# A hybrid decoder block: the input also comes transposed, and its row blocks are no longer turned by TensorE

## The chip, the cores and the metric

The kernel runs on one core of one Trainium2 chip. The metric is the device time of one execution in microseconds (us). A core has five engines that run their own instruction streams in order: TensorE (PE; its weight loads are shown as PEld), VectorE (DVE), ScalarE (ACT), GpSimd (POOL) and SyncE (SP), which here issues nearly all DMAs. They wait for one another by semaphores.

## The reference, cut to what matters

The block takes x of 4096 tokens by 1024 features in float32. Only its first step is touched by the change:

```
h    = x * rsqrt(mean(x*x, axis=-1) + 1e-6) * attn_norm      # row factor, then a gain per feature
proj = h @ w_in                                              # 1024 x 4104, split into q, k, v, gates, ...
o_a  = gated_delta_net(...)    # heads 0..3, chunks along the sequence
o_b  = retention(...)          # heads 4..7
x    = x + concat(o_a, o_b) @ w_out
out  = final_norm(x + mixture_of_experts(rms_norm(x)))
```

The matrix product needs h with the features on the partitions (the contracted axis), while x lies in memory with the tokens as rows.

## The kernel before

The mixer works through the sequence in 8 superblocks of 512 tokens (T), each made of 4 row blocks of 128 tokens. A superblock has four stages, in the order a1, b1, a0, b0: "a" is a pair of DeltaNet heads, "b" a pair of retention heads, the digit is the pair. A stage has four groups of weight columns; each group's products come in four units, and a unit of a projection is 24 matmuls into one of two PSUM accumulators (`acc`, pool `pa`): 8 slices of the contraction by three terms, since both operands are split into a high and a low part (`hh`, `hl` for the input, `wh`, `wl` for the weights). In `proj_n` the block of 128 tokens is the stationary operand; in `proj_t` the weights are.

Order is written out by hand. After each unit, `unit` runs the steps that `STEPS` lists for its kind: E empties the accumulator (the evacuation), L takes the next step of the DeltaNet chain of the pair before (a generator, `gdn_pair`, whose pace per unit is `PLAN`), B takes one entry of the list `bg`, W and S load or split weights, T runs delayed work. In stage b0 the kinds are r (8 units, here r0 to r7), v (v0 to v3) and y (y0 to y3), with the orders `r="WEBLTS"`, `v="WSBLET"` and `y="WLETSB"`. Every engine takes its part of these steps in the order in which they are written.

Rows of x come in by `x_load` (three buffers `xi`). `x_norm` squares and sums a row block on ACT (L310), finishes the mean on DVE (L311), takes the power on POOL (L312), and returns a closure that multiplies the row block by its row factor and by `attn_norm`, spread over all partitions as `arow` (DVE, L313). `x_turn` turns the block by 8 transposes on TensorE into two PSUM tiles (L320), copies each half into `hh` on ACT (L322), and forms `hl` as the difference on DVE (L323). For the blocks of the next superblock these steps go through `bg`: in b0, `bg` gets `x_norm`, scale for three blocks (six entries, one per unit from r0 on); their `x_turn` come after y1, y2 and y3; the fourth block is normed in units y3 and a0 of the next stage a1 and turned ahead of a1's third projection. The first superblock's rows go through `setup`, between the first four projections.

`split` makes the two parts of a quarter of a weight group (L144 on ACT, L145 on DVE) in the first superblock and stores them in DRAM (`wsp`); later superblocks read them back. After the mixer come the output projection and the experts, which the change leaves alone.

Of the kernel before, what the change touches and what calls it, by code (L numbers as in the profile page):

```python
# [8 lines left out]
F32 = mybir.dt.float32  # L9
# [3 lines left out]
AF = mybir.ActivationFunctionType  # L13
# [4 lines left out]
P = 128  # L18
# [42 lines left out]
def rows(ap, off, pat):  # L61
    return bass.AP(tensor=ap.tensor, offset=ap.offset + off, ap=pat)
# [3 lines left out]
    return ctx.enter_context(tc.tile_pool(name=name, bufs=bufs, reuse_waits="tile", **kw))  # L66


def mixer(tc, outer, banks, x, attn_norm, w_in, conv_a, a_log, dt_bias, norm_a, norm_b, cst, rope, mixed, clear, w_out, x1, wsp):


    nc = tc.nc
# [5 lines left out]
    with ExitStack() as ctx:  # L78
# [8 lines left out]
        ones = C[:, C_UT + P - 1:C_UT + P].to_broadcast([P, P])  # L87
        neg = C[:, C_NEG:C_NEG + P]
        pcol = cp.tile([P, 48], F32, name="pcol")
        arow = mp.tile([P, D], F32, name="arow")  # L90
        nrow = cp.tile([P, 128 + 512 + 8], F32, name="nrow")
        nega = cp.tile([P, 4], F32, name="nega")
        dtb = nrow[:, 644:648]
# [34 lines left out]
        def split(m):  # L128

            if m < len(quarters):  # L130
                src, c0, n, k = quarters[m]
                if m < M0 + 8:
                    t = wp.tile([P, 4 * 264], F32R, name="wq", bufs=NWH)[:, :4 * n]
                    keep = rows(wsp, m % MS * P * 4 * 264, [[4 * 264, P], [1, 4 * n]])
                    h, l = (t[:, 2 * i * n:2 * i * n + 2 * n].rearrange("p (k c) -> p k c", k=2) for i in range(2))
                    whs[m], wls[m] = h, l
                if MS <= m < M0:
                    nc.sync.dma_start(t.bitcast(F32), keep)
                    fetch(m + NWR)
                    return  # L140
                r = raws.pop(m)[:, :, :n]
                if m >= M0 + 8:
                    h, l = (t[:, 2 * k:2 * k + 2, c0 - T:c0 - T + n] for t in out.second)
                nc.scalar.activation(h, r, AF.Copy)  # L144
                nc.vector.tensor_tensor(l, r, h.bitcast(F32), op=OP.subtract)  # L145
                if m < MS and NS > 1:
                    nc.sync.dma_start(keep, t.bitcast(F32))
                if src is w_out and m < M0 + 8:
                    out.first[k, c0 // 256] = h, l
            fetch(m + NWR)  # L150
# [145 lines left out]
            return rest  # L296


        xs = {}

        def x_load(r):
            if r < S // P:
                xs[r] = row()
                nc.sync.dma_start(xs[r], rows(x, r * P * D, [[D, P], [1, D]]))

        def x_norm(r):
            if r < S // P:
                xi, st = xs[r], sp.tile([P, 2], F32, name="st")
                jx = mp.tile([P, D], BF, name="jx", bufs=1)
                nc.scalar.activation(jx, xi, AF.Square, accum_out=st[:, 0:1])  # L310
                nc.vector.tensor_scalar(st[:, 0:1], st[:, 0:1], 1.0 / D, EPS, op0=OP.mult, op1=OP.add)  # L311
                nc.gpsimd.tensor_tensor(st[:, 1:2], st[:, 0:1], ex[:, 0:1], op=OP.pow)  # L312
                return lambda: nc.vector.scalar_tensor_tensor(xi, xi, st[:, 1:2], arow, op0=OP.mult, op1=OP.mult)  # L313

        def x_turn(r):
            i, xi = r % NT, xs.pop(r)
            for q in range(2):
                tr = ptr.tile([P, 4, P], F32, name="tr")
                for j in range(4):
                    nc.tensor.transpose(tr[:, j], xi[:, (4 * q + j) * P:(4 * q + j + 1) * P], ident)  # L320
                sl = (slice(None), slice(4 * q, 4 * q + 4), slice(i * P, i * P + P))
                nc.scalar.activation(hh[sl], tr, AF.Copy)  # L322
                nc.vector.tensor_tensor(hl[sl], tr, hh[sl].bitcast(F32), op=OP.subtract)  # L323

        def next_rows(r):
            if NT <= r < S // P and r in xs:
                x_turn(r)
                x_load(r + NXI)
                if r % NT == 0:
                    bg[:0] = [lambda: None] + x_prep(r + NXI)  # L330

        def x_prep(r):

            box = []
            return [lambda: box.append(x_norm(r)), lambda: box[0] and box[0]()]

        def decays(ba):
            co = gp.tile([P, 14, 16], F32, name="co")
# [53 lines left out]

        L = dict(locals())
        with tc.manual_schedule():
            x_load(0)
            nc.sync.dma_start(ident, cst[:, C_ID:C_ID + P])
            nc.sync.dma_start(arow, rows(attn_norm, 0, [[0, P], [1, D]]))
            nc.gpsimd.memset(ex[:, 0:8], -0.5)
            nc.gpsimd.memset(ex[:, 8:16], 0.5)
            for m in range(NWR):  # L400
# [14 lines left out]
            x_turn(0)  # L415
            for m in range(4):
                split(m)
            scale = x_norm(1)
            split(4)

            def setup(i):

                if i:
                    x_turn(i)
                if i < NT - 1:
                    bg.append(scale if i == 0 else x_norm(i + 1))
                if i == 0:
                    nc.vector.tensor_scalar(nrow[:, :640], nrow[:, :640], 0.5, None, op0=OP.mult)
                    nc.scalar.activation(nega, nrow[:, 640:644], AF.Exp)
                    nc.vector.tensor_scalar(nega, nega, -1.0, None, op0=OP.mult)  # L430
                if i == NT - 1:
                    pp = ptr.tile([P, 512], F32, name="tr")
                    nc.tensor.transpose(pp[:, :48], prow, ident[:48, :48])
                    nc.vector.tensor_copy(pcol, pp[:, :48])
                x_load(i + NXI)
# [1314 lines left out]


def body(tc, x, attn_norm, w_in, conv_a, a_log, dt_bias, norm_a, norm_b, w_out, ffn_norm, wrg, wre,
         w_gate, w_up, w_down, final_norm, cst, rope, cst2, out, parts=7):
    S = x.shape[-2]
    with tc.tile_pool(name="dr", bufs=1, space=DRAM) as dp:
        mixed = dp.tile([S, D], F32, name="mixed")
        x1 = dp.tile([S, D], F32, name="x1")
        tab = dp.tile([NEXP * (S + P), 8], F32, name="tab")
        info = dp.tile([P, 2 * NOV + 1], F32, name="info")
        wsp = dp.tile([64, P, 2, 2, 264], F32, name="wsp")  # L1760
        with ExitStack() as right, ExitStack() as banks, ExitStack() as left:
            o = mixer(tc, left, banks, x, attn_norm, w_in, conv_a, a_log, dt_bias, norm_a, norm_b, cst, rope, mixed, (tab, out),
                      w_out, x1, wsp)
            sh = Shared(tc, pool(tc, right, "sh", 1, side="right"), cst2, ffn_norm, final_norm)
            experts = moe(tc, w_gate, w_up, w_down, sh, x1, tab, info, out)

            def then():
                left.close()
                if parts & 4:
                    next(experts)  # L1770

            if parts & 2:
                post(tc, o, wrg, wre, sh, tab, then)
            banks.close()
            if parts & 4:
                for _ in experts:
                    pass
# [23 lines left out]
```

## Time and profile before

| what | value |
|---|---|
| median of 3 runs | 3530.3 us (3528.6 to 3532.85) |
| the profiled execution | 3531.7 us, of which 3529.9 us is the span from its first to its last instruction |
| TensorE busy | 3373.2 us of the span |
| VectorE busy | 2166.1 us |
| mean granted TensorE clock | 0.986 |

How to read the profile's lines: a timeline line has the start, the length, the engine, the source line, the operation, the tile written and the tile read, the shape and the number of merged instructions; in brackets is the engine's idle time ahead of it and what ended that. Matmuls are pipelined, so their recorded lengths overlap: what one costs is the distance between starts.

### The profile page before, as it was taken

How to read it: one execution, taken by the hardware profiler on the slowest of the kernel's cores; microseconds unless marked ns; L12 is line 12 of the kernel's file. 1: busy time of each engine (PE TensorE's matmuls, PEld its weight loads, DVE VectorE, ACT ScalarE, POOL GpSimd, SP SyncE). 2: the span in 40 equal slices, each digit the busy share in tenths (PEclk: the TensorE clock that was granted, in tenths of full speed). 3: DMA queues.
4: the chain of work that ended last, by engine and by line, in shares of the span. 5: the costliest groups of instructions: out<-in, count | busy, mean ns of one | idle time of the engine just before them, and what ended most of it. 6: DMA issues, size and time to landing. Idle time of an engine off the chain costs nothing. (4 is left out here: it accounts for less than half of the span.)

```text
span 3529.9 us, 64890 instructions
## 1 busy us (share of the span) xinstructions
PE 3373.2 (96%) x24177; PEld 3090.6 (88%) x24177; DVE 2166.1 (61%) x5718; ACT 1502.5 (43%) x3322; POOL 1012.8 (29%) x1320
## 2 busy tenths in 40 slices
PE   7999999999999999999999999999789999999996
PEld 6989999999999999899999988888678888888785
DVE  5685576476466566556655735444556776777775
ACT  4344243233333333333332323222245666766775
POOL 1222232232232222222222211111223444444553
PEclk9999999999999999999999999999889999999998
DMA  8766446455454455464464444323368898899995
GB/s 273 218 241 199 150 152 208 156 161 194 163 184 165 163 175 172 151 206 151 164 209 141 138 157 139 120 97 120 118 203 267 290 314 294 308 325 329 329 321 190
DMA packets 463372, 710.95 MB, mean 201 GB/s; under 512 B 151328, under 2 KB 342480, under 8 KB 463056
## 3 DMA queue, kind: packets, MB, share of 16 engines
q1 hardware_dynamic: 426688, 622.03, 53.4%
q0 software_dynamic: 34976, 84.20, 6.7%
q8 instruction: 191, 3.13, 0.4%
q14 instruction: 125, 1.02, 0.1%
q10 hardware_dynamic: 1392, 0.56, 0.1%
HBM read 606.19 MB, written 131.99 MB: 209 GB/s over the span
## 5 line engine op out<-in xcount | busy, mean ns | idle before, releaser
L243 PE MATMUL acc<-wq,hh 128*128 128x256 f32 (+1 forms) x2560 | 751.1, 293 | 38.5 <-DVE rb L839 23.5
L245 PE MATMUL acc<-wq,hl 128*128 128x256 f32 (+1 forms) x2560 | 724.1, 283 | 2.1 <-DVE hl L323 2.1
L244 PE MATMUL acc<-wq,hh 128*128 128x256 f32 (+1 forms) x2560 | 724.6, 283 | 0.2 <-DVE wq L145 0.2
L243 PEld LDWEIGHTS acc<-wq,hh 128*128 128x128 f32 x2560 | 487.5, 190 | 49.3 <-issue 26.5
L245 PEld LDWEIGHTS acc<-wq,hl 128*128 128x128 f32 x2560 | 485.8, 190 | 2.8 <-DVE hl L323 2.8
L244 PEld LDWEIGHTS acc<-wq,hh 128*128 128x128 f32 x2560 | 487.4, 190 | 0.6 <-DVE wq L145 0.5
L231 PE MATMUL acc<-hh,wq 128*128 128x512 f32 x768 | 317.7, 414 | 0.4 <-DMA wq<-wsp 0.4
L233 PE MATMUL acc<-hh,wq 128*128 128x512 f32 x768 | 302.0, 393 | 0.0
L232 PE MATMUL acc<-hl,wq 128*128 128x512 f32 x768 | 300.9, 392 | 0.0
L1612 PEld LDWEIGHTS g<-xT,gu 128*128 128x128 f32 x2048 | 273.5, 193 | 15.7 <-DVE xT L1544 6.0
L1612 PE MATMUL g<-xT,gu 128*128 128x128 f32 (+30 forms) x2048 | 279.0, 295 | 3.4 <-DVE xT L1544 3.2
L1612 PE MATMUL u<-xT,gu 128*128 128x128 f32 (+30 forms) x2048 | 275.9, 293 | 0.0
L1612 PEld LDWEIGHTS u<-xT,gu 128*128 128x128 f32 x2048 | 266.3, 191 | 1.9
L271 DVE SCALAR_TENSOR_TENSOR cv<-xin,pcol,cv 128x512 f32<-128x512 f32 x288 | 216.3, 751 | 73.5 <-ACT cv L269 66.4
L279 POOL TENSOR_TENSOR gs<-gs,nrow 128x256 f32<-128x256 f32 x128 | 97.0, 758 | 543.6 <-DVE gs L278 517.5
L840 POOL TENSOR_TENSOR rqk<-rqk,rb 128x256 f32<-128x256 f32 x128 | 115.8, 905 | 250.6 <-DVE rb L839 178.9
L966 PE MATMUL y<-dh,hh 128*128 128x512 f32 (+16 forms) x400 | 163.9, 410 | 24.3 <-ACT ys L1555 15.0
L1587 POOL DMA_INDIRECT out_dram<-xg,mi x100 | 131.4, 1314 | 189.7 <-DVE ss L1583 96.3
L1555 ACT ACTIVATE ys<-y,mf 128x512 f32<-128x512 f32 (+22 forms) x200 | 133.8, 680 | 115.1 <-PE y L968 114.2
L233 PEld LDWEIGHTS acc<-hh,wq 128*128 128x128 f32 x768 | 144.2, 188 | 32.9
L1558 POOL DMA_INDIRECT xg<-out_dram,mi x97 | 98.2, 1013 | 255.9 <-PE tr L1542 47.0
L288 POOL TENSOR_TENSOR ss<-ss,ex 128x2 f32<-128x2 f32 x128 | 101.4, 792 | 238.3 <-DVE ss L287 205.1
(375 smaller groups left out, 7905.3 us busy)
## 6 DMA issues: line engine op xcount, KB each, us to landing
wq<-wsp SPq DMA_DIRECT2D x420, 512.0 KB, 5.5
gu<-in_w_gate_dram SPq DMA_DIRECT2D x128, 512.0 KB, 6.4
gu<-in_w_up_dram SPq DMA_DIRECT2D x128, 512.0 KB, 7.9
dn<-in_w_down_dram SPq DMA_DIRECT2D x64, 1024.0 KB, 10.2
xi<-in_x_dram SPq DMA_DIRECT2D x64, 512.0 KB, 5.2
wsp<-wq SPq DMA_DIRECT2D x60, 512.0 KB, 4.3
mixed<-mx SPq DMA_DIRECT2D x128, 128.0 KB, 2.3
out_dram<-zt SPq DMA_DIRECT2D x8, 2048.0 KB, 17.1
```

The lines of the kernel that those rows point to most:

```text
L231: nc.tensor.matmul(a, wh[:, s], hh[:, k, :], start=(k == 0), stop=False)
L232: nc.tensor.matmul(a, wh[:, s], hl[:, k, :], start=False, stop=False)
L233: nc.tensor.matmul(a, wl[:, s], hh[:, k, :], start=False, stop=(k == KC - 1))
L243: nc.tensor.matmul(a[:, :n], hh[:, k, s], wh[:, :n], start=(k == 0), stop=False)
L244: nc.tensor.matmul(a[:, :n], hh[:, k, s], wl[:, :n], start=False, stop=False)
L245: nc.tensor.matmul(a[:, :n], hl[:, k, s], wh[:, :n], start=False, stop=(k == KC - 1))
L271: nc.vector.scalar_tensor_tensor(cv, xin[:, j:j + T], tap(j), cv, op0=OP.mult, op1=OP.add)
L840: nc.gpsimd.tensor_tensor(o.rearrange("p h s d -> p (h s d)"), o.rearrange("p h s d -> p (h s d)"), b.rearrange("p h s d -> p (h s d)"), o ...
L966: nc.tensor.matmul(out, a.hi, b.hi, start=(i == 0), stop=False)
L1555: nc.scalar.activation(self.y[:R, s], y[:R], AF.Copy, scale=self.f[:R, WT, self.n:self.n + 1])
L1587: so = nc.gpsimd.indirect_dma_start(out=orow, out_offset=self.idx(0), in_=self.xg[:self.G], in_offset=None, bounds_check=S - 1, oob_is_err ...
L1612: nc.tensor.matmul(o[:, b, :R], self.w.gu[k // 4][:, k % 4, i * DE + b * P:i * DE + b * P + P], self.xT[:, k, :R], start=(k == 0), stop=(k ...
```

## The change

The host adds `xt`, the same input with each block of 128 tokens transposed: for each block, 128 partitions (feature within a slice of 128) by 8 slices by 128 tokens. `x_load` now reads `xt`. The row factors still need the rows, so `r_load` reads x as well, into one buffer `xr`; each `x_norm` issues the load of the next row block behind its own square. The closure now spreads the 128 row factors over all partitions by one matmul (the factor column, broadcast, against the identity) into a PSUM tile, and multiplies the transposed block by it. `x_turn` only splits. `attn_norm` comes as `acol`, features on partitions, and is multiplied into the weights in `split`, slice by slice. In `bg` the entries of a row block are now `x_norm`, nothing, scale: nine for three blocks in b0, so scales fall on r2, r5 and v0 (before: r1, r3, r5), and the fourth block's entries begin in y2.

```diff
-        arow = mp.tile([P, D], F32, name="arow")
+        acol = cp.tile([P, KC], F32, name="acol")
...
-                nc.scalar.activation(h, r, AF.Copy)
-                nc.vector.tensor_tensor(l, r, h.bitcast(F32), op=OP.subtract)
+                if m < MS:
+                    for i in range(2):
+                        a = acol[:, 2 * k + i:2 * k + i + 1]
+                        nc.scalar.activation(h[:, i], r[:, i], AF.Copy, scale=a)
+                        nc.vector.scalar_tensor_tensor(l[:, i], r[:, i], a, h[:, i].bitcast(F32), op0=OP.mult, op1=OP.subtract)
+                else:
+                    nc.scalar.activation(h, r, AF.Copy)
+                    nc.vector.tensor_tensor(l, r, h.bitcast(F32), op=OP.subtract)
...
-                nc.sync.dma_start(xs[r], rows(x, r * P * D, [[D, P], [1, D]]))
+                nc.sync.dma_start(xs[r], rows(xt, r * P * D, [[D, P], [1, D]]))
+        def r_load(r):
+            if r < S // P:
+                xr[r] = mp.tile([P, D], F32, name="xr")
+                nc.sync.dma_start(xr[r], rows(x, r * P * D, [[D, P], [1, D]]))
...
-                nc.scalar.activation(jx, xi, AF.Square, accum_out=st[:, 0:1])
+                nc.scalar.activation(jx, xr.pop(r), AF.Square, accum_out=st[:, 0:1])
+                r_load(r + 1)
                 nc.vector.tensor_scalar(st[:, 0:1], st[:, 0:1], 1.0 / D, EPS, op0=OP.mult, op1=OP.add)
                 nc.gpsimd.tensor_tensor(st[:, 1:2], st[:, 0:1], ex[:, 0:1], op=OP.pow)
-                return lambda: nc.vector.scalar_tensor_tensor(xi, xi, st[:, 1:2], arow, op0=OP.mult, op1=OP.mult)
+                def scale():
+                    tr = ptr.tile([P, 4, P], F32, name="tr")
+                    nc.tensor.matmul(tr[:, 0], st[:, 1:2].to_broadcast([P, P]), ident, start=True, stop=True)
+                    xi = xs[r].rearrange("p (k t) -> p k t", k=KC)
+                    nc.vector.tensor_tensor(xi, xi, tr[:, 0:1].to_broadcast([P, KC, P]), op=OP.mult)
+                return scale
         def x_turn(r):
-            i, xi = r % NT, xs.pop(r)
+            i, xi = r % NT, xs.pop(r).rearrange("p (k t) -> p k t", k=KC)
             for q in range(2):
-                tr = ptr.tile([P, 4, P], F32, name="tr")
-                for j in range(4):
-                    nc.tensor.transpose(tr[:, j], xi[:, (4 * q + j) * P:(4 * q + j + 1) * P], ident)
-                sl = (slice(None), slice(4 * q, 4 * q + 4), slice(i * P, i * P + P))
-                nc.scalar.activation(hh[sl], tr, AF.Copy)
-                nc.vector.tensor_tensor(hl[sl], tr, hh[sl].bitcast(F32), op=OP.subtract)
+                k = slice(4 * q, 4 * q + 4)
+                sl = (slice(None), k, slice(i * P, i * P + P))
+                nc.scalar.activation(hh[sl], xi[:, k], AF.Copy)
+                nc.vector.tensor_tensor(hl[sl], xi[:, k], hh[sl].bitcast(F32), op=OP.subtract)
...
-                    bg[:0] = [lambda: None] + x_prep(r + NXI)
+                    bg[:0] = x_prep(r + NXI)
...
-            return [lambda: box.append(x_norm(r)), lambda: box[0] and box[0]()]
+            return [lambda: box.append(x_norm(r)), lambda: None, lambda: box[0] and box[0]()]
...
+            r_load(0)
+            nc.sync.dma_start(ident, cst[:, C_ID:C_ID + P])
+            nc.sync.dma_start(acol, rows(attn_norm, 0, [[1, P], [P, KC]]))
             x_load(0)
-            nc.sync.dma_start(ident, cst[:, C_ID:C_ID + P])
-            nc.sync.dma_start(arow, rows(attn_norm, 0, [[0, P], [1, D]]))
...
-            scale = x_norm(1)
+            scales = [x_norm(1)]
             split(4)
             def setup(i):
                 if i:
                     x_turn(i)
-                if i < NT - 1:
-                    bg.append(scale if i == 0 else x_norm(i + 1))
+                if scales:
+                    scales.pop(0)()
+                if i + 2 < NT:
+                    scales.append(x_norm(i + 2))
```

## Rows read from the trace of the kernel before

**Rows 1.** The page, part 1: busy time, share of the span, instructions.
```profile
PE 3373.2 (96%) x24177; PEld 3090.6 (88%) x24177; DVE 2166.1 (61%) x5718; ACT 1502.5 (43%) x3322; POOL 1012.8 (29%) x1320
```
**Rows 2.** Busy time by stretch (us, instructions), then granted clock, DMA share, GB/s.
```profile
0.00:44.00 44.00, 25.15 (x131) 22.61 (x132) 19.86 (x34) 15.66 (x29) 5.81 (x17) 0.88 0.82 273
44.00:258.00 214.00, 206.53 (x1464) 192.12 (x1463) 163.30 (x426) 98.35 (x261) 53.74 (x76) 0.98 0.73 234
...
1538.00:1794.00 256.00, 252.38 (x1906) 237.80 (x1906) 157.57 (x452) 90.04 (x276) 67.59 (x103) 1.00 0.53 170
```
**Rows 3.** Waits of TensorE from 44 to 2030 us: total, times, longest.
```profile
PE acc L243 <- DVE rb L839: 23.5, 18, 2.2
PE acc L243 <- DVE gs L278: 6.7, 8, 3.1
```
**Rows 4.** Timeline of TensorE, units y0 to y3 of b0, seventh superblock.
```profile
1766.00 0.61 PE L882 MATMUL sm<-qkt 128*128 128x128 f32 x4
1766.37 0.37 PE L243 MATMUL acc<-wq,hh 128*128 128x256 f32 x1
...
1767.88 1.03 PE L320 MATMUL tr<-id,xi 128*128 128x128 f32 x8
1769.25 0.39 PE L243 MATMUL acc<-wq,hh 128*128 128x256 f32 x1 [0.34 <-DVE gs L278]
...
1774.43 1.04 PE L320 MATMUL tr<-id,xi 128*128 128x128 f32 x8
1775.22 0.36 PE L243 MATMUL acc<-wq,hh 128*128 128x256 f32 x1
```
**Rows 5.** Timeline of VectorE, units r5 to y0 of the same b0.
```profile
1745.15 0.37 DVE L836 TENSOR_TENSOR rqk<-acc,rt 128x256 f32<-128x256 f32 x1
...
1745.84 1.26 DVE L313 SCALAR_TENSOR_TENSOR xi<-xi,st,arow 128x1024 f32<-128x1024 f32 x1
1747.04 0.70 DVE L723 TENSOR_SCALAR tk<-tk 128x8 f32<-128x8 f32 x1
...
1749.78 0.41 DVE L836 TENSOR_TENSOR rqk<-acc,rt 128x256 f32<-128x256 f32 x1
...
1750.50 2.88 DVE L732 SCALAR_TENSOR_TENSOR V<-U,V 128x31 f32<-128x31 f32 x12
...
1768.81 0.38 DVE L278 SCALAR_TENSOR_TENSOR gs<-th,acc 128x256 f32<-128x256 f32 x1
```
**Rows 6.** Timeline of the last superblock's b0, VectorE, then TensorE.
```profile
1996.12 0.15 DVE L723 TENSOR_SCALAR tk<-tk 128x8 f32<-128x8 f32 x1
...
2019.47 0.39 PE L243 MATMUL acc<-wq,hh 128*128 128x256 f32 x1 [1.63 <-DVE gs L278]
```
**Rows 7.** Timeline of the first 44 us.
```profile
11.87 0.59 PE L243 MATMUL acc<-wq,hh 128*128 128x264 f32 x1 [1.22 <-ACT wq L144]
...
13.11 0.34 SPq L410 DMA_DIRECT2D cst<-in_cst_dram  x1
...
14.41 1.06 ACT L310 ACTIVATE jx<-xi 128x1024 bf16<-128x1024 f32 x1 [0.65 <-DMA xi<-in_x_dram]
...
15.83 0.54 POOL L312 TENSOR_TENSOR st<-st,ex 128x1 f32<-128x1 f32 x1 [8.60 <-DVE st L311]
...
33.40 0.39 PE L243 MATMUL acc<-wq,hh 128*128 128x264 f32 x1 [0.52 <-ACT hh L322]
...
43.70 0.40 PE L231 MATMUL acc<-hh,wq 128*128 128x512 f32 x1
```
**Rows 8.** DMA time to landing of the row loads, first 50 us.
```profile
DMA to landing us min/median/max: 3.3/5.6/9.5
```
**Rows 9.** VectorE lines L145 and L323: length in ns min/median/max, first and last start.
```profile
L145 DVE TENSOR_TENSOR wq<-wr,wq x51: 671/686/1268, 60.3 to 252.8; 128x512 fp32r<-128x512 f32 x51
L323 DVE TENSOR_TENSOR hl<-tr,hh x64: 674/681/693, 10.5 to 1797.1; 128x512 fp32r<-128x512 f32 x64
```
**Rows 10.** Timeline of TensorE, first superblock's b0, start of y2.
```profile
262.25 0.39 PE L243 MATMUL acc<-wq,hh 128*128 128x256 f32 x1 [3.08 <-DVE gs L278]
```

More of the change, by code (lines that the diff above doesn't have):

```diff
@@ L66, in pool, with mixer @@
     return ctx.enter_context(tc.tile_pool(name=name, bufs=bufs, reuse_waits="tile", **kw))
-def mixer(tc, outer, banks, x, attn_norm, w_in, conv_a, a_log, dt_bias, norm_a, norm_b, cst, rope, mixed, clear, w_out, x1, wsp):
+def mixer(tc, outer, banks, x, xt, attn_norm, w_in, conv_a, a_log, dt_bias, norm_a, norm_b, cst, rope, mixed, clear, w_out, x1, wsp):
     nc = tc.nc
@@ L296, in norm_out @@
             return rest
-        xs = {}
+        xs, xr = {}, {}
         def x_load(r):
@@ L303, in x_load @@
                 xs[r] = row()
-                nc.sync.dma_start(xs[r], rows(x, r * P * D, [[D, P], [1, D]]))
+                nc.sync.dma_start(xs[r], rows(xt, r * P * D, [[D, P], [1, D]]))
[3 more added lines that the diff above has]
+                nc.sync.dma_start(xr[r], rows(x, r * P * D, [[D, P], [1, D]]))
         def x_norm(r):
             if r < S // P:
-                xi, st = xs[r], sp.tile([P, 2], F32, name="st")
+                st = sp.tile([P, 2], F32, name="st")
@@ L1752, in body @@
 def body(tc, x, attn_norm, w_in, conv_a, a_log, dt_bias, norm_a, norm_b, w_out, ffn_norm, wrg, wre,
-         w_gate, w_up, w_down, final_norm, cst, rope, cst2, out, parts=7):
+         w_gate, w_up, w_down, final_norm, cst, rope, cst2, xt, out, parts=7):
     S = x.shape[-2]
@@ L1761, in body @@
         with ExitStack() as right, ExitStack() as banks, ExitStack() as left:
-            o = mixer(tc, left, banks, x, attn_norm, w_in, conv_a, a_log, dt_bias, norm_a, norm_b, cst, rope, mixed, (tab, out),
+            o = mixer(tc, left, banks, x, xt, attn_norm, w_in, conv_a, a_log, dt_bias, norm_a, norm_b, cst, rope, mixed, (tab, out),
                       w_out, x1, wsp)
@@ L1791 @@
     arrays["cst2"] = constants2()
+    arrays["xt"] = np.ascontiguousarray(arrays["x"].reshape(S // P, P, KC, P).transpose(0, 3, 2, 1))
     arrays = {f"in_{n}_dram": a for n, a in arrays.items()}
```

## The prediction

> **What bounds the kernel now.** I read the busy times first, then busy time by stretch, then TensorE's own waits, and last the timeline where those waits fall. TensorE is busy for 96% of the span, VectorE for 61% [rows 1]: the first guess is that every microsecond taken from TensorE is a microsecond won. The stretches qualify that. A middle superblock has 256 us with 252.4 us of TensorE work at the full granted clock [rows 2], so some 3.6 us of idle time per superblock; the first 44 us hold only 25.2 us of work. TensorE's waits between 44 and 2030 us are nearly all for VectorE, to empty an accumulator [rows 3]. In the timeline the first kind sits in the r units (r7 waits for r5's accumulator in most superblocks), the second at y2, which starts 0.34 us after TensorE was ready, on the gate product `gs` of y0 [rows 4]. So there is a stretch in each b0, from the middle of the r units to the start of y2, whose length is set by VectorE; outside it, TensorE sets the pace. Both kinds of stretch hold a part of the change.
>
> **Price of the turns.** Eight transposes move the next projection by 0.79 us (1774.43 to 1775.22), and the first matmul behind a switch is recorded about 0.08 us longer: 0.87 us [rows 4]. A float32 matmul of the new one's shape shows as two records; four records take 0.37 us to the next start, with the switch 0.46 us, so one costs 0.23 us [rows 4]. On TensorE alone a row block gains 0.64 us; the 28 blocks behind the first superblock 17.9 us. That is one bound.
>
> **The steady state, block by block.** There are seven sets of four blocks, one per change of superblock.
>
> *Blocks two and three* are turned after y2 and y3, where VectorE is not late: minus 2 x 0.87 = 1.74 us. *Block four* is turned ahead of the third projection of a1: minus 0.87; its new matmul stands behind a1's first projection and is not covered: plus 0.23. The matmuls of blocks one to three stand behind r2, r5 and v0, inside the stretch that VectorE sets; their 0.69 us hides behind the waits of r7 and y2, and would be added if those waits were gone.
>
> *Block one* is turned after y1, just ahead of the start of y2, which waits for VectorE anyway [rows 4]. Taking these 0.87 us away only lengthens that wait; the last superblock, which has no such turn there, shows it: y2 waits 1.63 us instead of 0.34 [rows 6]. So y2 starts when `gs` of y0 is done, and VectorE is at work without a gap from r7's evacuation at 1749.78 to there, 1768.81 [rows 5]. What does the change do to this chain? The third scale moves from r5 to v0, into it. The r5 place is taken by the second scale, so r6 and r7 gain nothing and the chain grows by one multiplication, 1.26 us [rows 5]; the new one has the same 1,024 elements per partition, and I take that price. The third block's mean falls behind r6: 0.15 us more, the price of L723 [rows 6] as the nearest tiny operation. Against that, L723 took 0.70 us behind the old scale [rows 5] and 0.15 where no scale precedes it [rows 6]. The delay looks like a lock with POOL: the old scale reads two SBUF tensors, holds up POOL's sum of r5, and that sum holds up L723. The new scale reads one operand from PSUM; I take back 0.4 of the 0.55 us. Together y2 starts 1.0 us later; bounds 0.4 and 1.4.
>
> One set is then -1.74 - 0.87 + 0.23 + 1.0 = -1.38 us, seven sets -9.7 us. The bounds are -17.9 us (the chain is no limit) and, with 1.4 us on the chain and one blocked `hl` (next), -0.4 us a set: -2.7 us.
>
> `hl` now subtracts two SBUF tensors, where one came from PSUM. L145 has two and took up to 1.268 us where 0.686 is its median; L323, one from PSUM, stays within 0.693 [rows 9]. So up to 0.58 us can be added when POOL works at the same time. In y2 and y3 VectorE has room for it; ahead of a1's fourth projection it could reach TensorE: between nothing and 0.58 us a set. I take nothing, since the subtraction no longer waits for a turn and has the whole third projection, 24 matmuls, to run in. The Trainium skill says of this, in "SBUF — State Buffer", section "Who interferes with whom", that a VectorE instruction with two SBUF inputs contends with a GpSimd instruction that reads SBUF, and that the later one blocks. The trace agrees (1.268 against 0.693 us). By that rule alone, every fourth block's subtraction being caught, the seven sets would give -5.6 us in place of -9.7.
>
> **The first superblock.** Its 64 splits become two instructions each on ACT and VectorE. A half costs at least 0.38 us (the gate product of 256 columns [rows 5]), two 0.8 against 0.69 [rows 9]: about 0.13 us per split. This is hidden behind TensorE except in the stretches that VectorE sets: some eight splits in b1 and nine in b0, 1.0 and 1.2 us. In b0 y2 waits 3.08 us already [rows 10], so nothing there can be covered. Plus 2.2 us, bounds 0 and 4.
>
> **The start.** Before, the first projection began at 11.87 [rows 7], while the norm of block one came later and off TensorE's queue. Now the spreading matmul of block one stands in TensorE's queue ahead of that projection, and it needs the rows of block one, whose load SP issues behind all the setup loads (13.11 is the last [rows 7]), at 13.5 or later. It lands 5.6 us later by the median of such loads [rows 8], at about 19.5. From the square's start to the end of the power it takes 1.96 us (14.41 to 16.37 [rows 7]): the matmul runs at about 21.5, the projection ends near 27. Block two's rows are loaded only after block one's square and behind the stores of the split weights, near 21, landing near 27; its matmul is ahead of the second projection, which so starts near 30. Block three's load follows block two's square, lands near 33.5, and its matmul can run near 35.5, in front of the third projection; by the pace of projections and splits this comes at 37.5, where it was 33.40 before [rows 7]. From there on the pace is the old one: the transposed products begin at about 48 instead of 43.70 [rows 7]. Queued behind the waiting squares on ACT are the evacuations and splits, already counted; behind `r_load` on SP, which waits for each square, the next weight loads. Plus 4.5 us. With 3.3 us for each landing the same chain gives +0.5, with 9.5 us +12 [rows 8]. The load of `acol` (4 KB in pieces of 4 bytes) is covered by the wait for block one's rows; without this cover it would be on the way of the first split.
>
> In the steady state the doubled input (16.8 MB more) goes into queues at half their share [rows 2] and lands within three units, some 9 us; ACT has room. I cost it at nothing; if a load were later than that, ACT would stand in its square and the evacuations of the v and y units behind it.
>
> **The sum.** -9.7 + 2.2 + 4.5 = -3.0 us against the profiled execution's 3531.7 us: 3528.7. That execution lies 1.4 us above the median of the runs, so I forecast 3527.3 us.
>
> **Rivals.** 0.2% is 7 us, about what a measurement of this kernel can tell from no change.
>
> *TensorE is the bound everywhere*: VectorE's chain has slack that I don't see (a cheaper scale, fewer locks with POOL), and the four turns pay in full. For it: 96%. Against it: y2's waits [rows 4, 6, 10]. -17.9 + 4.5 + about 1 = -12.4: 3518 us, faster.
>
> *The start decides against it*: each of the three row loads lands as late as the latest, since the queues are full in the first 44 us (share 0.82 [rows 2]): +12 there, and the chain in b0 at its upper bound, -2.7 + 4: +13, 3543 us, slower. It decides from landing times of some 8 us on, with the chain at that bound. Against it: the median of 5.6.
>
> *VectorE's chain takes nearly all*: y2 is 1.4 us later and `hl` blocked, with the start as forecast: -2.7 + 2.2 + 4.5 = +4, 3534 us, no change that can be told.
>
> **Chances.** My forecast 0.40, TensorE everywhere 0.27, the chain takes all 0.18, the start 0.15. Some of the forecast's own spread reaches past -7 us (about 0.08), and some of the start's stays under +7. Faster by over 0.2%: 0.33; within: 0.49; slower: 0.18. The likeliest case's own range is 3522 to 3533; the range that takes in the rivals, but not the whole of the start's, is 3515 to 3540 us.
>
> **What would show it.** Right: y2's wait for `gs` grows from 0.34 us to about 2.2; y3 and a1 follow with no turn; a superblock is shorter by 1.4 us; the 512-column products begin at 46 to 50 us, TensorE's first projection near 21. Wrong: superblocks shorter by 2.5 us, or y2's start not tied to `gs` of y0; a start before 45 us; new waits of TensorE for POOL (row factors) or of ACT for the row load in the middle.

## The result, and the profile after

The changed kernel takes 3559.65 us (median of 6 runs, 3557.07 to 3564.64), the kernel before 3530.1 us beside it: a ratio of 1.0083, 95% interval 1.0072 to 1.0094. It is 29.5 us slower; the forecast was 3527.3 us, with 3540 us as the upper end.

The page of the changed kernel, part 1, answers to [rows 1]:

```profile
PE 3370.9 (95%) x23985; PEld 3084.7 (87%) x23985; DVE 2180.8 (61%) x5782; ACT 1521.2 (43%) x3386; POOL 993.0 (28%) x1320
```

TensorE is busy for 2.3 us less and the kernel is 30 us longer, so most of the loss lies in waits; busy time also grows where the granted clock is lower, since the same products then take longer (in the first stage, matmuls of 264 columns start 0.22 us apart at a clock of 0.50 and 0.12 us apart at 1.00). VectorE, which had slack, has 15 us more to do. Busy time by stretch, cut at the changed kernel's own stages, answers to [rows 2]:

```profile
0.00:56.00 56.00, 22.39 (x106) 20.41 (x107) 20.49 (x41) 18.15 (x37) 6.63 (x17) 0.85 0.80 260
56.00:280.00 224.00, 209.40 (x1477) 194.16 (x1477) 178.75 (x491) 113.60 (x319) 51.93 (x77) 0.98 0.74 237
1552.00:1808.00 256.00, 249.15 (x1864) 234.27 (x1862) 158.31 (x453) 88.91 (x270) 63.53 (x100) 0.99 0.55 178
```

The first stage is 12 us longer with less TensorE work in it. A middle superblock, where 1.4 us less was forecast, has more idle time than before, and its granted clock is 0.99 where it was 1.00. TensorE's waits from 56 to 2040 us say for whom (total, times, longest; before in [rows 3]):

```profile
PE acc L250 <- DVE rb L859: 21.4, 19, 2.4
PE acc L238 <- DMA wq<-wsp: 21.1, 6, 4.1
PE acc L250 <- DVE gs L285: 16.6, 8, 4.5
```

The third line is the wait at y2, longer by 10 us in all, as forecast. The second is new: before, the first 512-column product waited for weights once, for 0.4 us in all; now it waits in six of the eight superblocks, 3.5 us on average. The forecast had no such wait.

**A ledger.** Two moments stand in both traces: the first 512-column product (L231 before, L238 after) and the start of y2 in each b0.

| from, to | before | after | difference | forecast |
|---|---|---|---|---|
| begin to the first 512-column product | 43.70 | 55.94 | +12.2 | +4.5 |
| to y2 of the first superblock (262.25; 279.35) | 218.6 | 223.4 | +4.9 | +2.2 |
| to y2 of the last, seven superblocks (2019.47; 2057.31) | 1757.2 | 1778.0 | +20.7 | -9.7 |
| the rest of the span | 1510.4 | 1505.5 | -4.9 | 0 |

The sum is +32.9, the two profiled executions' difference (3564.64 and 3531.7 us). The change touches nothing in the last row's work, and I have no cause for its 4.9 us; over the traces of this case that do the whole computation it lies between 1500.6 and 1510.4 us, and the kernel before with only its fills moved has 1507.4. The third row is the one to explain.

**Where the new wait comes from.** SyncE's timeline in a1 of the seventh superblock. The first fence is the kernel before, which was not shown for this engine; there y2 started at 1518.27:

```profile
1532.20 0.33 SPq L304 DMA_DIRECT2D xi<-in_x_dram  x1
...
1533.06 0.56 SPq L632 DMA_DIRECT2D tab<-zt  x1
1533.67 5.66 SPq L632 DMA_DIRECT2D out_dram<-zt  x1
1539.37 11.04 SPq L138 DMA_DIRECT2D wq<-wsp  x4
```

The same place in the changed kernel, where y2 started at 1556.91:

```profile
1572.76 0.33 SPq L311 DMA_DIRECT2D xi<-in_xt_dram  x1
...
1573.62 0.56 SPq L652 DMA_DIRECT2D tab<-zt  x1
1574.23 5.67 SPq L652 DMA_DIRECT2D out_dram<-zt  x1
1579.99 11.15 SPq L138 DMA_DIRECT2D wq<-wsp  x4
```

SyncE's order is the same: the next row block (`x_load`), the rope table, the zero fills of `tab` and `out_dram`, the weights of a1. Only the head comes later: 15.9 us behind y2 instead of 13.9. `x_load` waits until the buffer `xi` of block three is free. Before, its last reader was the transpose; now it is VectorE's subtraction `hl`, which ends later. The timelines show it, TensorE before, then VectorE in the changed kernel:

```profile
1531.13 1.04 PE L320 MATMUL tr<-id,xi 128*128 128x128 f32 x8
```

```profile
1570.87 1.86 DVE L340 TENSOR_TENSOR hl<-xi,hh 128x512 fp32r<-128x512 f32 x2
```

The turns end at 1532.17 and the load goes out at 1532.20; the subtractions end at 1572.73 and the load goes out at 1572.76. (The profile's table of SyncE's waits puts this wait, 4.1 us, down to the product `Sb` at L895. That began at 1572.66 and ended at 1573.07, behind the load's issue, so it cannot have released it.)

So the load of a block that is wanted a superblock later holds up the fills, and the fills stand ahead of weights that are wanted at once. TensorE, meanwhile, is ready earlier: it begins the first 512-column product 32.1 us behind this y2, where it was 34.3 before. It meets the missing weights here:

```profile
1593.21 0.50 PE L238 MATMUL acc<-hh,wq 128*128 128x512 f32 x1 [2.59 <-DMA wq<-wsp]
```

and pays again behind it. In the busy time by stretch of these microseconds the column to read is the granted clock, the number behind the last bracket:

```profile
1592.00:1594.00 2.00, 0.79 (x3) 0.67 (x4) 0.00 (x0) 0.00 (x0) 0.00 (x0) 1.00 0.98 379
1594.00:1596.00 2.00, 2.00 (x9) 1.69 (x7) 0.00 (x0) 0.00 (x0) 0.00 (x0) 0.53 1.01 346
1596.00:1598.00 2.00, 2.00 (x8) 1.62 (x7) 1.54 (x8) 0.00 (x0) 0.00 (x0) 0.61 1.06 406
1598.00:1600.00 2.00, 2.00 (x13) 1.70 (x12) 1.69 (x11) 0.29 (x1) 0.00 (x0) 1.00 1.02 416
```

TensorE stands still for 2.6 us and then runs near the lower level (1.2 GHz) for most of 4 us: about 1.7 us more lost (0.47 and 0.39 of 2 us each). The Trainium skill describes this pattern in "TensorE: Matmul & The Clock Gate", section "HAM oscillation — how this bites in real kernels": a wait for a transfer between groups of matmuls is paid a second time by a slow start of the next group. The rows here agree.

The last superblock of the same trace is a check: no row block is left to load there, the fills go out 12.6 us behind y2 instead of 16.7 to 18.3, and TensorE does not wait for weights.

### The profile page after: what moved, and what is told of

Same layout as the page of the kernel before. It is cut to its first block, busy times and chain, and to the rows that moved or that the text cites. A ratio compares the mean times of both kernels' runs of the same rounds, so it can differ in the third digit from the quotient of the medians.

```text
span 3562.8 us, 64769 instructions
## 1 busy us (share of the span) xinstructions
PE 3370.9 (95%) x23985; PEld 3084.7 (87%) x23985; DVE 2180.8 (61%) x5782; ACT 1521.2 (43%) x3386; POOL 993.0 (28%) x1320
## 5 line engine op out<-in xcount | busy, mean ns | idle before, releaser
L238 PE MATMUL acc<-hh,wq 128*128 128x512 f32 x768 | 323.5, 421 | 21.1 <-DMA wq<-wsp 21.1
L240 PE MATMUL acc<-hh,wq 128*128 128x512 f32 x768 | 306.0, 398 | 0.0
L238 PEld LDWEIGHTS acc<-hh,wq 128*128 128x128 f32 x768 | 147.9, 193 | 50.4 <-DMA wq<-wsp 23.7
L240 PEld LDWEIGHTS acc<-hh,wq 128*128 128x128 f32 x768 | 146.9, 191 | 34.2
L239 PEld LDWEIGHTS acc<-hl,wq 128*128 128x128 f32 x768 | 148.1, 193 | 25.6
```

Of the source, the lines that this page charges most:

```text
L238: nc.tensor.matmul(a, wh[:, s], hh[:, k, :], start=(k == 0), stop=False)
L239: nc.tensor.matmul(a, wh[:, s], hl[:, k, :], start=False, stop=False)
L240: nc.tensor.matmul(a, wl[:, s], hh[:, k, :], start=False, stop=(k == KC - 1))
```

## The experiments

The theory (A): in the steady state the loss is the late release of `xi`, through SyncE's order, and nothing else; without it the forecast's -1.4 us per superblock is there. The main rival (B): the second input copy loads the queues so much that weights come late wherever they stand. A second question is the start, a third what is left to win. The kernel before was run again beside each group of runs, with medians from 3526.64 to 3529.11 us; each ratio is to the median beside it. In the texts written ahead of the runs, e1 is the changed kernel with the fills out of the way, e3 the one with the load behind the fills, f1 the one with the rows ahead.

**The fills out of the way**, in the changed kernel and, as control, in the kernel before:

```
-  if (kind, pr) == (("a", 1) if sb else ("a", 0)):
+  if (kind, pr) == (("b", 1) if sb else ("a", 0)):
```

> The changed kernel with one line different: from the second superblock on, the zero fills of the output and the table are issued at the start of stage b1 instead of a1. Theory A (late weights): SP's load of the next transposed block now waits for VectorE's subtraction of block three; the 2.5 MB of fills and then the weights of a1's first 512-column group stand behind it on SP, so TensorE waits some 3.5 us there in six superblocks and then runs some microseconds at the lower clock. Then both go: the six waits (21.1 us) are gone, the middle superblocks take 249.3 us instead of 255.0, the kernel 3525 us (3520 to 3530). Rival B (the second row load and SP's waits for the squares are the load): the fills are not the cause, at least half of the waits stay, 3545 us or more. Rival C (the loss per superblock is VectorE's chain at y2): the superblocks stay at 255, 3560 us.

> The kernel before with the same move of the zero fills, as a control. A: there the weights came just in time (one wait of 0.4 us in all), so moving the fills gives nothing: 3530 us, within 2 us. If moving the fills by itself were worth tens of microseconds, e1 would not speak for A: then 3510 or less.

Measured: the changed kernel 3530.34 us against 3526.64 beside it (ratio 1.0008, 0.9999 to 1.0018), the kernel before with the same edit 3530.53 us (1.001, 1.0001 to 1.002). Of the 29.5 us, 3.7 are left, and the interval of the ratio takes in 1; the time is just above the 3520 to 3530 us that was expected. TensorE's waits for weights fall from 21.1 to 1.2 us, and the six superblocks between the first y2 and the seventh take 249.7 us instead of 255.0. The control shows that moving the fills is no gain by itself (they then hold up weights in the last superblock's b1, 1.7 us of waits in its trace). With the same edit, the two kernels are level.

**The load behind the fills**, which keeps the fills where they were:

```
+ if r % NT == 2: held.append(r + NXI)
+ else: x_load(r + NXI)
  ...
  for t in clear: zero(nc, t, zt, sb, NS)
+ while held: x_load(held.pop())
```

> The changed kernel; the fills stay at a1, but the load that waits for block three's subtraction is issued behind them. Same DMAs, same bytes, another order on SP. A: the fills and the weights no longer wait for VectorE, the six waits go, 3527 us (3520 to 3533). B: nothing changes, since the same bytes are moved: 3560 us.

Measured: 3528.55 us (ratio 1.0007, 0.9997 to 1.0016). SyncE in the seventh superblock's a1; the y2 before it was at 1522.79:

```profile
1536.91 0.56 SPq L658 DMA_DIRECT2D tab<-zt  x1
1537.52 5.42 SPq L658 DMA_DIRECT2D out_dram<-zt  x1
1543.04 9.58 SPq L312 DMA_DIRECT2D xi<-in_xt_dram  x1
1552.72 1.82 SPq L138 DMA_DIRECT2D wq<-wsp  x4
```

The fills go out 14.1 us behind y2 instead of 16.7 (12.6 to 14.2 over the superblocks), and the last weights' issue ends 31.8 us behind it instead of 34.2, though a load now stands between them. No wait of TensorE for weights is left before 2080 us. The seven superblocks from y2 to y2 take 1743.9 us: 13.3 less than before, 34.1 less than in the changed kernel. That is 13 us more than the 21.1 us of waits, and the granted clock is where they were: in the changed kernel, stretches of 8 us from each of the six waits on had a mean clock of 0.57 (four times) or 0.79 (twice). The share that is missing adds up to 17 us, a part of it while TensorE still stood, which covers the 13. The edit keeps every transfer and every byte; only the order on SyncE is another.

**The kernel before without the turns.** The eight transposes are left out and ACT and VectorE split the untransposed rows, so the numbers are others; no second layout, no second load, 256 transposes fewer:

```
- for j in range(4):
-     nc.tensor.transpose(tr[:, j], xi[:, (4 * q + j) * P:(4 * q + j + 1) * P], ident)
+ tr = xi[:, 4 * q * P:(4 * q + 4) * P].rearrange("p (k t) -> p k t", k=4)
```

> The kernel before with its 256 turns simply left out (the split reads the rows where they are, so the products are those of other numbers); no second load, no spreading matmul, scales where they were. It shows what taking the turns away is worth at most. A: block buffers are released by the subtraction here too, so the weights of a1 come late as well: waits of 2 to 3.5 us in the middle superblocks and a lower clock behind them; of the 24 us of turns little is left, 3520 to 3540 us. B: without the second load no waits, 3508 us.

Measured: 3546.76 us (ratio 1.005, 1.0033 to 1.0067): slower, with work taken away and nothing added. TensorE's waits, 60 to 2080 us,

```profile
PE acc L231 <- DMA wq<-wsp: 22.0, 6, 4.4
```

and VectorE and SyncE ahead of the seventh superblock's fills, the y2 before them at 1540.73:

```profile
1555.73 1.29 DVE L321 TENSOR_TENSOR hl<-xi,hh 128x512 fp32r<-128x512 f32 x2 [0.36 <-ACT hh L320]
1557.05 0.33 SPq L304 DMA_DIRECT2D xi<-in_x_dram  x1
```

`x_load` now goes out when `hl` ends, as in the changed kernel, 16.3 us behind y2, where it went out when the transposes ended before, and the wait for weights appears in full, six times, with one input copy: B falls. The time is 7 us above A's own range. And y2 waits 1.1 to 1.3 us instead of 0.34, as the forecast said of a turn taken from ahead of y2: the time only moves into the wait.

**The rows ahead.** From here each kernel contains the load behind the fills unless it says otherwise. The rows of blocks one to three go early into tiles that are idle then (`at`, `X`, `U`), and each is loaded ahead of its transposed block:

```
+ early = {1: ('at', 8), 2: ('X', 8), 3: ('U', 8)}
  ...
  for r in range(1, min(NXI, NT)):
+     r_load(r)
      x_load(r)
```

> The kernel of e3 (late load behind the fills) with the rows of blocks one to three loaded early at the start, into buffers that are idle then, each ahead of its transposed block, instead of each behind the square of the block before. Theory A (the start is lost to three row loads in series): the first 512-column product begins at 44 to 48 us instead of 55.9, and the kernel is 8 to 11 us faster than e3, some 3519 us. Rival B (the start is lost to split weights, to the bytes themselves or to the clock): the start stays above 52 us and the time within 3 us of e3.

Measured: 3524.05 us (ratio 0.9985, 0.9975 to 0.9994), 4.5 us less than without, or 6 by the kernel before beside each; the first 512-column product begins at 49.67 instead of 52.96. That is about half of what was expected, and the timelines of ACT and TensorE say why:

```profile
22.73 0.91 ACT L148 ACTIVATE wq<-wr,acol 128x256 fp32r<-128x256 f32 x2 [7.52 <-DMA wr<-in_w_in_dram]
23.55 1.04 ACT L328 ACTIVATE jx<-X 128x1024 bf16<-128x1024 f32 x1
...
26.21 0.79 PE L338 MATMUL tr<-id,st 128*128 128x128 f32 x2 [4.90 <-POOL st L334]
```

Block two's rows, issued at 7.25, are no longer what the square waits for; it stands on ACT behind a split of weights, for which ACT stood idle 7.5 us. The wait was pushed from one load to the next.

**The scale one entry earlier.** Block scales sit two entries of the work list behind their norms, and the third falls into VectorE's chain ahead of y2. This puts them one entry behind, and the empty entry in front of the list:

```
- return [lambda: box.append(x_norm(r)), lambda: None, lambda: box[0] and box[0]()]
+ return [lambda: box.append(x_norm(r)), lambda: box[0] and box[0]()]
- bg[:0] = x_prep(r + NXI)
+ bg[:0] = [lambda: None] + x_prep(r + NXI)
```

> The kernel of e3 with the empty entry taken out between norm and scale, so that the scales fall on r1, r3 and r5 as before the change. Theory A (the third scale at v0 lengthens VectorE's chain ahead of y2): y2's wait falls from 1.93 us to 0.9 to 1.3 us and the kernel gains 4 to 7 us on e3, 3523 us. Rival B (the matmul then waits for the power on POOL, one unit earlier): TensorE gets waits for POOL of about a microsecond, three per superblock, and the gain is gone or turned: 3528 us or more.

Measured: 3563.14 us (ratio 1.0102, 1.0085 to 1.0119): 35 us slower than without, a plain miss. TensorE's waits, 60 to 2080 us, and SyncE ahead of the seventh superblock's fills (the y2 before them at 1555.02):

```profile
PE acc L238 <- DMA wq<-wsp: 21.2, 6, 4.8
PE tr L330 <- POOL st L326: 19.2, 8, 3.3
PE acc L250 <- DVE gs L285: 13.7, 9, 4.5
```

```profile
1569.50 0.33 SPq L317 DMA_DIRECT2D xr<-in_x_dram  x1
...
1570.36 0.56 SPq L658 DMA_DIRECT2D tab<-zt  x1
```

y2 waits 1.1 us instead of 1.9, the gain meant. Two things cost more. The spreading matmul, now straight behind the norm, waits 2.5 us for GpSimd's power once in each superblock. And the empty entry moved a row load behind one more square; it holds the fills until 15.3 us behind y2 instead of 14.1, and the six waits for weights are back. The same fault as in the change, made by another load. To part the two costs, the same edit on the changed kernel with the fills in b1, so that no fill stands ahead of those weights:

> The changed kernel with each block's scale one entry of the work list behind its norm, as in the run that put the scales there (3563.1 us), but with the zero fills in the next group of products instead of the first 512-column group (as in the run with the fills moved, 3530.3 us). Question: why did the scale one entry earlier cost 35 us? Theory A, two parts: (1) the empty entry in front moved a row load behind a square and with it the fills (1.2 us later against y2) and the weights (six waits, 21.2 us together, each with some us of low clock behind it: about 34 us by the runs with and without these waits); (2) TensorE now waits 2.5 us once in a superblock at the spreading matmul for GpSimd's power and 0.8 us less at y2. Here (1) is gone and (2) stays: no wait of TensorE for wq over 1.5 us before 1800 us, 7 to 8 waits of 2.5 us for st, y2 waits of 1.1 us, superblocks of 250.5 to 251.5 us, 3538 us (3533 to 3543). Theory B (the waits for GpSimd's power are all of it): 3560 us. Theory C (the weights are all of it, the 2.5 us are given back): 3525 us, superblocks of 248.5.

Measured: 3538.85 us (ratio 1.0031, 1.002 to 1.0041), by theory A 3538. The same waits, 60 to 2080 us:

```profile
PE tr L329 <- POOL st L325: 19.2, 8, 3.3
...
PE acc L250 <- DMA wq<-wsp: 2.8, 3, 1.8
```

The waits for GpSimd stay, those at L238 go, and 24 of the 35 us with them. The rest is 8.5 us over the kernel with the fills moved alone by the medians, and 9.3 between the first and the last y2 of the traces (1755.4 and 1746.1). Seven times 2.5 less 0.8 would be 12; why some of it does not show was not looked into.

**The splits as before**, with attn_norm left out of the weights, so that the numbers are others; the later stages depend on them (the whole took 3740.3 us, which compares with nothing), and only the first superblock is read:

```
- if m < MS:
+ if False:
```

> The kernel of e3 with the weights split as before, in one instruction on each engine; attn_norm is left out of the computation. It prices the gain in the weights. Theory A: 0.13 us for each of some seventeen splits that lie in the stretches set by VectorE in the first superblock: 2.2 us faster than e3, the wait of y2 there 3.3 us instead of 4.47. Rival B: the split is hidden altogether, the wait stays at 4.4 us.

Measured: from the first 512-column product to y2 of the first superblock 217.0 us (57.11 to 274.10), against 223.6 us with the split halves; TensorE's waits there are 11.0 us instead of 14.8. Busy time by stretch, with the split halves, then without:

```profile
52.96:276.54 223.58, 208.77 (x1474) 193.54 (x1472) 178.56 (x490) 113.09 (x317) 50.56 (x76) 0.98 0.74 237
57.11:274.10 216.99, 206.01 (x1473) 190.75 (x1472) 165.76 (x434) 98.07 (x261) 51.45 (x76) 1.00 0.76 243
```

So the split halves cost 6.6 us there, where the forecast had 2.2: 3.8 us of waits, and 2.8 us more of TensorE's busy time for the same products, at a granted clock of 0.98 instead of 1.00. The wait of y2 fell only to 4.12 us, not to the 3.3 expected; the rest of the 3.8 lies in the waits ahead of it. Against the kernel before (218.6) the rest of the change gives back 1.6 us.

**The norms in a0.** With the rows ahead, the norms and scales of the next superblock's first three blocks start from a0 instead of b0, one stage earlier and away from VectorE's chain:

```
  gs = []
+ if pr == 0:
+     for r in range(min(NXI, NT)): bg += x_prep(4 * sb + 4 + r)
  ...
- if pr == 0:
-     for r in range(min(NXI, NT)): bg += x_prep(4 * sb + 4 + r)
```

> The kernel of f1 with the norms and scales of the next superblock's first three blocks moved from stage b0 to stage a0. Theory A (VectorE sets the length of b0 from the r units to y2): with three scales and means out of it, the waits of r7 and y2 shrink, the middle superblocks take 247 us or less instead of 249.3, and the kernel is 10 to 18 us faster than f1, some 3505 us. Rival B (a0 has no room, its convolutions fill VectorE): TensorE gets new waits in a0 and nothing is won.

Measured: 3518.18 us (ratio 0.9971, 0.9959 to 0.9982): faster than the kernel before and the changed one, but 5.9 us under the run with the rows ahead, where 10 to 18 were expected; the six middle superblocks take 248.6 us, not 247. TensorE's waits, 60 to 2080 us:

```profile
PE acc L250 <- DVE rb L874: 15.2, 12, 2.4
PE acc L250 <- DVE gs L285: 13.0, 9, 3.8
PE acc L250 <- DVE tk L758: 8.6, 8, 2.4
PE acc L238 <- DMA wq<-wsp: 2.7, 2, 1.4
```

The waits for `gs` and `rb` fall by 11.5 us against the run with the rows ahead (18.2 and 21.5), and 7.7 us of that come back as waits for `tk`. With the fills in b1 on top:

> The fastest version so far (rows of the first blocks early, the load behind the fills, the norms of the next superblock begun in a0: 3518.2 us) with the zero fills in the next group of products as well. Theory A (a weight load that waits behind the fills costs the wait and a low clock behind it): the two waits of 1.3 us for wq that are left there go, 3515 us (3511 to 3519). Theory B (they cost nothing more than 2.7 us, or the fills hurt in their new place too): 3518 us or more, with waits for wq in b1.

Measured: 3516.13 us (ratio 0.9963, 0.9949 to 0.9976). The waits at L238 are gone, 2.3 us of others stand in b1; the two versions can't be told apart, their intervals overlap.

## Why the prediction was wrong

**The step that failed** is the price of the removed turns together with that of the loads in the steady state. The transposes were priced as TensorE's time alone; they were also what set `xi` free, and their removal put the release on VectorE's `hl`. The loads were put at nothing ("I cost it at nothing; if a load were later than that, ACT would stand in its square"): that sentence asked whether bytes find room in the queues, and where a late load would be missed. It didn't ask what a load itself waits for, and what stands behind it on SyncE. The forecast named what is queued behind `r_load`'s wait, and not what is behind `x_load`'s. In place of nothing the traces showed six waits for weights, 21.1 us together, and about 13 us more at the lower clock behind them; the times put it at 27.6 us of the 29.5: the changed kernel is 29.5 us above the kernel before beside it, the one with the load behind the fills 1.9. The kernel before without its turns shows the same waits without the rest of the change, so the second input copy is not their cause.

**The steady state without this step: the sum right, its pieces in part by luck.** With the load behind the fills a superblock takes 249.1 us on average against 251.0: -1.9 us, forecast -1.4, bounds -0.4 to -2.6. Cut at two waits of TensorE for `rb` that stand in both traces, the long one in b1 and the one at r7 of b0 (means over the superblocks):

| from, to | before | load behind the fills | difference | forecast |
|---|---|---|---|---|
| y2 to the long wait in b1 | 104.4 | 102.8 | -1.5 | -2.4 |
| to r7 of b0 | 123.8 | 122.8 | -1.0 | 0 |
| to y2 | 23.0 | 23.6 | +0.6 | +1.0 |

The first row holds the turns of blocks two to four. In four of the seven superblocks it is 102.1 to 102.4 us, close to the forecast; in the other three the granted clock falls behind y2, whose wait is now longer, and 1.5 us are lost, a term that the forecast didn't have. In the second row "r6 and r7 gain nothing" failed. VectorE behind r3 and TensorE at r7 in the seventh superblock, before:

```profile
1735.79 2.62 DVE L665 SCALAR_TENSOR_TENSOR E<-E,co,cst 128x128 f32<-128x128 f32 x4
1746.06 0.36 PE L243 MATMUL acc<-wq,hh 128*128 128x256 f32 x1 [1.55 <-DVE rb L839]
```

and with the load behind the fills:

```profile
1739.60 1.62 DVE L691 SCALAR_TENSOR_TENSOR E<-E,co,cst 128x128 f32<-128x128 f32 x4
1748.97 0.36 PE L250 MATMUL acc<-wq,hh 128*128 128x256 f32 x1 [0.64 <-DVE rb L865]
```

The same four products take 1.0 us less where no scale stands ahead of them at r3, and r7's product starts earlier by as much: the forecast counted such a delay for L723 behind r5, and not for these. So y2 starts 0.4 us earlier against the wait in b1, where 1.0 us later was forecast, while the first row gained less than forecast; that the two nearly cancel is luck. Other pieces, in the timelines of VectorE and TensorE, b0 of the changed kernel's sixth superblock:

```profile
1541.57 1.21 DVE L331 TENSOR_TENSOR xi<-xi,tr 128x1024 f32<-128x1024 f32 x1
...
1556.91 0.39 PE L250 MATMUL acc<-wq,hh 128*128 128x256 f32 x1 [1.90 <-DVE gs L285]
```

The third scale stands inside VectorE's chain, as said, at 1.21 us (price taken: 1.26); the product behind the old scale's place takes 0.15 to 0.23 us where 0.70 stood in [rows 5], so about all of the 0.55 us came back, not 0.4; and y2 waits 1.90 us, forecast 2.2. The rival that TensorE sets the pace everywhere falls with this wait. `hl` with two SBUF operands was caught more often than "every fourth": its mean is 0.92 us with the load behind the fills (54 subtractions between 280 and 2000 us, up to 1.27 us), where L323 had 0.693 at most in [rows 9]. Of the 54, 27 take 0.83 us or more, and each of them overlaps an instruction of GpSimd in the trace; the 20 that overlap none take 0.68. But no wait of TensorE for it shows behind the start, so "nothing" was right for its price.

**The first superblock: a term too small.** +4.9 us, forecast +2.2 with bounds 0 and 4. The split was priced by the gate product at 0.38 us a half (twice that is 0.76, which against 0.69 gives 0.07 us per split, not the 0.13 written). Measured, by groups of the changed kernel from 0 to 280 us, VectorE:

```profile
L149 DVE SCALAR_TENSOR_TENSOR wq<-wr,acol,wq 128x256 fp32r<-128x256 f32 x120 | 58.3, 529 | 12.8 <-ACT wq L148 12.8
```

Two halves on VectorE take 1.06 us, where the whole took 0.76 on average before (the 60 of the same stage), so 0.30 us per split, not 0.13; by the forecast's own 17 uncovered splits that is 5.1 us, and the run with the splits as before measured 3.8 us of waits and 2.8 at a lower clock, 1.6 of which other parts of the change give back. The nearest row read one operand from PSUM, and these read two from SBUF: their median is 0.48 us, so the row taken was already too cheap. The longest half is 0.97 us. The section of the Trainium skill that the prediction weighed for `hl` ("SBUF — State Buffer", "Who interferes with whom") bears on this instruction too, since it has two operands in SBUF. The trace agrees: the 12 halves of 0.95 to 0.97 us all overlap an instruction of GpSimd, and the 81 that overlap none take 0.53 us at most.

**The start: its order right, its size off.** +12.2 us, forecast +4.5, bounds +0.5 and +12. The rival on the start had this price, but by three late loads, and only one of the three was late. The changed kernel's first 56 us, SyncE, ACT and TensorE:

```profile
14.03 0.33 SPq L316 DMA_DIRECT2D xr<-in_x_dram  x1
18.95 1.06 ACT L322 ACTIVATE jx<-xr 128x1024 bf16<-128x1024 f32 x1 [5.27 <-DMA xr<-in_x_dram]
20.96 0.80 PE L329 MATMUL tr<-id,st 128*128 128x128 f32 x2 [13.51 <-POOL st L325]
21.65 0.82 SPq L316 DMA_DIRECT2D xr<-in_x_dram  x1
31.23 1.06 ACT L322 ACTIVATE jx<-xr 128x1024 bf16<-128x1024 f32 x1 [8.83 <-DMA xr<-in_x_dram]
33.42 0.79 PE L329 MATMUL tr<-id,st 128*128 128x128 f32 x2 [7.70 <-POOL st L325]
...
43.22 0.39 PE L250 MATMUL acc<-wq,hh 128*128 128x264 f32 x1 [1.82 <-ACT hh L339]
```

Block one goes as written: issue 14.03 (13.5 said), matmul 20.96 (21.5). Block two is issued at 21.65 (21) and its square starts 9.6 us later, at 31.23, where 27 was said: the longest landing of [rows 8], not the median. Block three's load lands nearly in time: ACT waits 0.9 us for it. From there the third projection begins at 43.22 instead of 37.5, and the products 12.7 us behind it, not 10.3 as before. "By the pace of projections and splits" failed there, since the pace has the granted clock in it: it was 1.00 from 34 us on before, and in the changed kernel, whose projections stand between waits, it is 0.50 from 34 to 40 us, 0.53 from 46 to 48 and 0.50 from 52 to 54.

The first 512-column product's time is 52.5 to 57.6 us in the changed kernel and its versions that load rows as it does, so up to 5 us of the 12.2 vary from one execution to another.

**The sum with measured terms**, for the version with the load behind the fills: +9.3 at the start, +5.0 in the first superblock, -13.3 in the seven others is +1.0 us. The rest of its span is 6.7 us shorter than before, again without a cause that I know, so the two profiled executions differ by -5.8 us, while its median stands 1.9 us above the kernel before. So without the failed step no change could have been told, and the time would have been in the likeliest case's own range; but the three terms were each off by 3 to 5 us and cancelled, which is luck.

## What to carry to other kernels

When an instruction is removed, ask what it released: the buffer's next load now waits for the next-later reader, and everything issued behind that load on the same queue is late with it, even transfers that the change doesn't touch. Price a moved or added load three times: its bytes, what it waits for, and what stands behind it. And a new wait of TensorE is best priced above its length, by rows that show the granted clock behind a wait.

## What the runs showed of the hardware

The six waits for weights were 21.1 us and their removal gave 34.1 us over the same superblocks: behind the wait shown above (2.6 us) the clock was 0.53 and 0.61 for 4 us. The length of a wait alone does not tell what follows: behind the wait of 1.90 us at the y2 before it the clock was 1.00 (1556.9 to 1564.9 us), and behind the wait of 1.97 us one superblock earlier it was 0.79 on average (1300.6 to 1308.6 us). Fills that start 15.3 to 16.9 us behind y2 instead of 12.6 to 14.2 (the scale one entry earlier, against the load behind the fills) were enough to turn no wait for weights into six of 2.7 to 4.8 us. Both effects were larger than I would have put them.
